# An attention whose TensorE order is written out in steps: score bank, third transposes, weighted sum, projections, second score bank, first two transposes

## The chip, the cores and the metric

The kernel runs on one NeuronCore of a Trainium2 chip. The metric is the device time of one execution in microseconds (us). Three executions of the kernel before took 912.99, 913.64 and 913.80 us; the median is 913.64 us. The profile is of one more execution.

## The reference, cut to what matters

Two layers over 1040 tokens (16 meta tokens and 1024 real ones) with 1024 features: a multi-head latent attention, then a recurrent mixer. Only the attention is touched by the change. For each of 8 heads it computes

```
s = (einsum('bqhd,bkhd->bhqk', qn, k_nope) + einsum('bqhr,bkr->bhqk', qr, k_rope)) * scale
s = where(mask, s, MASK_VALUE)          # causal
p = softmax(s, axis=-1)
out = einsum('bhqk,bkhd->bqhd', p, v)
y = out.reshape(B, T, MLA_WIDTH) * silu(gate)
return y @ w_out
```

where q, k and v are projections of normalised latents (384 features for q, 256 for k and v).

## The kernel before

**Precision.** Nearly every product is made of three matmuls in the type fp32r on a high and a low part of each operand (`mm3`: high*high, high*low, low*high). So each result that feeds another product is copied out of PSUM by ScalarE (`hi_of`, the high part), and VectorE then writes the difference (`lo_of`, the low part). A PSUM bank is free for the next product when that difference is done.

**Stages.** Input projection and gate come first (to about 206 us in the trace), then the attention (206 to 513 us), then the output projection and the second layer.

**The attention.** A head is cut into 9 blocks of 116 queries (`QBLK`, the last has 112); a unit is (head h, block t), 72 units in all. Names in the trace:

- `pk`, `pqn`, `pv`: the projections `k_unit`, `q_unit`, `v_unit`. Keys and queries come in chunks of 348 tokens, three to a head, values in 9 blocks for a pair of heads. They share two PSUM banks (tag "g") with the weighted sum `o`, and become `kh`/`kl`, `qh`/`ql`, `v`.
- `s`: `scores(h, t)`, five matmuls for each segment of keys, up to two segments in a tile of two banks; there are two such tiles (tag "s2"). Only t = 8 needs a second tile (1040 keys in three segments), so `s..8_0` and `s..8_1` take both. VectorE adds the causal mask and takes the row minimum `m`; ScalarE writes the exponential `p` out of the tile (L523), which frees it. For t = 8 the minimum spans both tiles, so neither exponential starts before `s..8_1` is done. There are three buffers of `p`, so the exponential of unit u+3 also waits for the transposes of unit u.
- `pt`: `transposes(h, t)` turns `p` over in groups of up to three 116x116 transposes, a group to each chunk of keys (one group for t = 0 to 2, two for 3 to 5, three for 6 to 8). There are two banks for groups (tag "t"). ScalarE and VectorE copy a group to `pth` and `ptl`; a bank is free after `ptl`.
- `o`: `weighted(h, g)`, once after every third unit, 9, 18 or 27 matmuls over a chunk of 348 queries.

**Order.** The loop runs over the units: scores of the unit three ahead (`LEAD`), a pending weighted sum, the projections that a table assigns to this unit (`fill`), the transposes of this unit. It only states dependencies and priority: a scheduler that knows the program places the instructions of every engine, and TensorE executes them in that order. It pulls pieces apart: between the matmuls of one weighted sum stand scores, transposes and projections. At odd heads `load_pair` also brings the projection weights of the next two heads, which ScalarE and VectorE split (`h_wkv`, `h_wq`, `l_wq`); `h_wq` goes into the buffer of the old weights, so it can only start when the last `pqn` of the pair has read them. In head 7 there is no next head; instead the output weights `wa` are split and three tiles of the output projection (`ao`) are placed there.

**At the start**, `k_unit(0,0)`, `k_unit(0,1)`, `q_unit(0,0)` follow each other, and ScalarE loads its table for exponentials behind the last gate.

Of the kernel before, what the change touches and what calls it, by code (L numbers as in the profile page):

```python
# [62 lines left out]
def trunk(ctx, tc, x, meta, a_norm_g, a_w_in, a_q_g, a_kv_g, a_w_uq, a_w_ukv, a_w_out,  # L63
# [18 lines left out]
    def lo_of(dst, src, hi):  # L82
        return nc.vector.tensor_tensor(dst, src, bc(hi), ALU.subtract)  # L83

    def mm3(ps, lh, ll, rh, rl, start, stop, **kw):
        nc.tensor.matmul(ps, lh, rh, start=start, stop=False, **kw)  # L86
        nc.tensor.matmul(ps, lh, rl, start=False, stop=False, **kw)  # L87
        return nc.tensor.matmul(ps, ll, rh, start=False, stop=stop, **kw)  # L88

    def mm_stack(ps, xp, k, n, wh, wl):  # L90
        if k:
            nc.tensor.matmul(ps[:n], xp[:, k, :n], wl, start=False, stop=False)
        nc.tensor.matmul(ps[:STK + n], xp[:, k], wh, start=k == 0, stop=k == KT - 1)
        if not k:
            nc.tensor.matmul(ps[:n], xp[:, k, :n], wl, start=False, stop=False)

# [70 lines left out]
    def transpose_in(xn, n, t0, xth, xtl, name):  # L167
        for j in range(2):
            pt = ps_t(f"xt_{name}_{j}")
            pv = pt.rearrange("p (a b) -> p a b", b=P)[:, :, :n]  # L170
            for a in range(4):
                k = 4 * j + a
                nc.tensor.transpose(pv[:, a], xn[:n, k * P:(k + 1) * P], ident[:n, :n])
# [120 lines left out]
    def lat_post(i, lt, krf):  # L294
        t0, n = TOK[i]
        pt = ps_t(f"qt{i}")
        pv = pt.rearrange("p (a b) -> p a b", b=P)[:, :, :n]
        for a in range(QKT):
            nc.tensor.transpose(pv[:, a], lt[:, a * P:(a + 1) * P], ident[:n, :n])
        nc.tensor.transpose(pv[:, 3], krf[:, 0:P], ident[:n, :n])  # L300
        hi_of(qlh[:, :, t0:t0 + n], pv[:, :3])
        lo_of(qll[:, :, t0:t0 + n], pv[:, :3], qlh[:, :, t0:t0 + n])
        nc.scalar.activation(ks1[:, t0:t0 + n], pv[:, 3], AF.Copy)
        pt = ps_t(f"kt{i}")
        pv = pt.rearrange("p (a b) -> p a b", b=P)[:, :, :n]
        for a in range(VKT):
            nc.tensor.transpose(pv[:, a], lt[:, QL + a * P:QL + (a + 1) * P], ident[:n, :n])
        nc.tensor.transpose(pv[:, 2], krf[:, DR:DR + P], ident[:n, :n])
# [19 lines left out]
    for c in range(0, D, 512):  # L328
        ps = ps_m(f"rb_ga{c}")
        nc.tensor.matmul(ps, ones, g_a[0:1, c:c + 512], start=True, stop=True)  # L330
        rbs.append(ps)
# [109 lines left out]
    def k_unit(h, c):  # L441
        if c == 0:
            KK[h] = (pat.tile([P, T], F32R, name=f"kh{h}", tag="kh", bufs=2),
                     pat.tile([P, T], F32R, name=f"kl{h}", tag="kl", bufs=2))
        kvw, hh = KV[h // 2], h % 2
        c0, cw = CH[c]
        ps = ps_g(f"pk{h}_{c}")[:, :cw]
        for k in range(VKT):
            last = mm3(ps, kvw[0][:, k, hh * 256:hh * 256 + DN], kvw[1][:, k, hh * 256:hh * 256 + DN],
                       klh[:, k, c0:c0 + cw], kll[:, k, c0:c0 + cw], k == 0, k == VKT - 1)  # L450
        kh, kl = KK[h]
        hi_of(kh[:, c0:c0 + cw], ps)
        lo_of(kl[:, c0:c0 + cw], ps, kh[:, c0:c0 + cw])
        return last

# [29 lines left out]
    def scores(h, t):  # L485
# [13 lines left out]
        for s, sg in enumerate(tiles):  # L499
            ps2 = ps_2(f"s{h}_{t}_{s}")  # L500
            w = sg[0][1]
            for j, (k0, w_) in enumerate(sg):
                assert w_ == w
                ps = ps2[:n, j, :w]
                nc.tensor.matmul(ps, a, kth[:, k0:k0 + w], start=True, stop=False)  # L505
                nc.tensor.matmul(ps, a, ktl[:, k0:k0 + w], start=False, stop=False)
                nc.tensor.matmul(ps, b_, kth[:, k0:k0 + w], start=False, stop=False)
                nc.tensor.matmul(ps, r_, ks1[:, k0:k0 + w], start=False, stop=False)
                nc.tensor.matmul(ps, r_, ks2[:, k0:k0 + w], start=False, stop=True)  # L509
# [23 lines left out]

    def transposes(h, t):
        g = t // 3
        b0, n = QBLK[t]
        off = b0 - CH[g][0]
        p = PP.pop((h, t))
        if t % 3 == 0:
            PT[h, g] = [(pat.tile([QB, GRP, CHW], F32R, name=f"pth{h}_{g}_{tr}", tag="pth", bufs=3),  # L540
                         pat.tile([QB, GRP, CHW], F32R, name=f"ptl{h}_{g}_{tr}", tag="ptl", bufs=3))
                        for tr in range(g + 1)]
        for tr in range(g + 1):
            pth, ptl = PT[h, g][tr]
# [3 lines left out]
            for j, kb in enumerate(kbs):  # L548
                k0, nk = QBLK[kb]
                nc.tensor.transpose(pv[:nk, j], p[:, k0:k0 + nk], ident[:n, :n])  # L550
            nfull = sum(1 for kb in kbs if QBLK[kb][1] == QB)
# [97 lines left out]
    for h in range(H):  # L649
        for c in range(len(CH)):  # L650
# [33 lines left out]
    for u in range(LEAD):  # L684
        scores(*units[u])
# [12 lines left out]
    st_at.close()  # L698
# [445 lines left out]
```

## Time and profile before

| what | us |
|---|---|
| median of three executions | 913.64 |
| profiled execution, whole time | 913.04 |
| its span on the core | 911.3 |
| TensorE (PE) matmuls busy in the span | 887.8 |
| VectorE (DVE) busy | 582.9 |
| ScalarE (ACT) busy | 467.7 |

The span is the time between the first and the last instruction; 1.7 us lie around it. PE is TensorE's matmul side, PEld its weight loads, POOL GpSimd and SP the queue that issues DMAs. A matmul's duration in the trace runs until its last result has left the array, so matmuls that follow each other overlap; the distance of their starts tells how long each holds the engine. The granted TensorE clock is a share of 2.4 GHz.

### The profile page before, as it was taken

The page shows a single profiled execution, that of the slowest core. Times are in us where ns is not written, and L with a number is a line of the kernel's source. Part 1 is how long each engine was busy: PE and PEld are TensorE (multiplying, and loading weights), DVE is VectorE, ACT ScalarE, POOL GpSimd, SP SyncE. Part 2 cuts the span into 40 slices and gives each one's busy share as a digit, 9 for nine tenths or more (in the row PEclk, how much of TensorE's full clock was granted, in tenths as well). Part 3 has the DMA queues.
Part 4 walks back from the last instruction along what each step waited for, and adds up shares of the span by engine and source line. Part 5 has one row for each costly group of instructions (what it writes and reads, how often), then busy time and mean ns, then how long its engine had stood idle before and what let it go on. Part 6 is the DMA issues. An engine that isn't in the chain of part 4 may idle for free.

```text
span 911.3 us, 13708 instructions
## 1 busy us (share of the span) xinstructions
PE 887.8 (97%) x5291; PEld 817.2 (90%) x5291; DVE 582.9 (64%) x1211; ACT 467.7 (51%) x942; POOL 43.6 (5%) x46
## 2 busy tenths in 40 slices
PE   7999999999999999999999999999999999999996
PEld 5999999999999999999988778799989989897885
DVE  6675423416677676676777357757393764868997
ACT  6543422224665655656656235634835457365455
POOL 3000000000000000000000000000020110312200
PEclk9999999999999999999999999999999999999998
DMA  7132345221010010010012424241111121237624
GB/s 275 48 87 64 85 110 158 73 72 40 16 57 16 17 55 16 17 63 16 17 37 103 163 92 159 101 75 48 46 47 51 43 58 36 95 90 231 141 68 184
DMA packets 71169, 72.25 MB, mean 79 GB/s; under 512 B 15056, under 2 KB 52688, under 8 KB 71104
## 3 DMA queue, kind: packets, MB, share of 16 engines
q1 hardware_dynamic: 68928, 67.19, 23.8%
q0 software_dynamic: 2176, 4.19, 2.6%
q8 instruction: 41, 0.67, 0.3%
q14 instruction: 24, 0.20, 0.1%
HBM read 58.65 MB, written 12.71 MB: 78 GB/s over the span
## 4 chain that ended last, share of the span: by engine, by line
PE 92%; ACT 3%; DVE 2%; issue 1%; DMA 0%; ACTq 0%; DVEq 0%
PE pt L550 4%; PE pu L88 3%; PE pu L86 3%; PE pu L87 3%; PE ga L86 3%; PE ao L86 3%; PE ga L87 3%; PE ga L88 3%; PE ao L88 3%; PE ao L87 3%; PE pg L87 3%; PE pg L88 3%; PE pg L86 3%; PE s L505 2%; PE b L86 2%; PE b L88 2%
## 5 line engine op out<-in xcount | busy, mean ns | idle before, releaser
L523 ACT ACTIVATE p<-s,m 116x116 f32<-116x116 f32 (+4 forms) x80 | 55.4, 694 | 45.1 <-DVE m L515 16.5
L80 ACT ACTIVATE pth<-pt 116x348 fp32r<-116x348 f32 (+5 forms) x152 | 57.1, 397 | 29.7 <-PE pt L550 26.2
L83 DVE TENSOR_TENSOR ptl<-pt,pth 116x348 fp32r<-116x348 f32 (+5 forms) x152 | 63.7, 437 | 9.7 <-ACT pth L80 9.2
L88 PE MATMUL pu<-x2h,l_wu 128*128 128x348 f32 (+1 forms) x192 | 61.5, 321 | 0.4 <-DVE l_wu L83 0.4
L86 PE MATMUL ga<-xth,h_wg 128*128 128x348 f32 (+1 forms) x192 | 61.9, 322 | 0.0
L86 PE MATMUL pu<-x2h,h_wu 128*128 128x348 f32 (+1 forms) x192 | 61.7, 322 | 0.0
L87 PE MATMUL pu<-x2l,h_wu 128*128 128x348 f32 (+1 forms) x192 | 61.7, 321 | 0.0
L87 PE MATMUL ga<-xtl,h_wg 128*128 128x348 f32 (+1 forms) x192 | 61.6, 321 | 0.0
L88 PE MATMUL ga<-xth,l_wg 128*128 128x348 f32 (+1 forms) x192 | 61.6, 321 | 0.0
L515 DVE CUSTOM_DVE_ANT_0 s<-s,maskt 116x116 f32<-116x116 f32 (+8 forms) x72 | 49.4, 686 | 16.9 <-PE s L509 16.6
L550 PE MATMUL pt<-ident,p 116*116 116x116 f32 (+1 forms) x360 | 54.0, 262 | 1.0 <-DVE ptl L83 0.6
L86 PE MATMUL ao<-wah,yh_a 128*128 128x512 f32 x128 | 50.5, 396 | 0.6 <-DVE Y L574 0.6
L87 PE MATMUL pg<-x2l,h_wbg 128*128 128x512 f32 x128 | 50.6, 395 | 0.0
L88 PE MATMUL pg<-x2h,l_wbg 128*128 128x512 f32 x128 | 50.3, 393 | 0.0
L86 PE MATMUL pg<-x2h,h_wbg 128*128 128x512 f32 x128 | 50.2, 392 | 0.0
L88 PE MATMUL ao<-wah,yl_a 128*128 128x512 f32 x128 | 50.2, 393 | 0.0
L87 PE MATMUL ao<-wal,yh_a 128*128 128x512 f32 x128 | 49.8, 390 | 0.0
L505 PE MATMUL s<-kh,qh 128*116 128x348 f32 (+7 forms) x120 | 42.0, 350 | 6.5 <-ACT p L523 6.5
L550 PEld LDWEIGHTS pt<-ident,p 116*116 116x116 f32 (+1 forms) x360 | 41.5, 135 | 4.0 <-PE pt L550 1.5
L87 PE MATMUL o<-ptl,v 116*128 116x348 f32 (+1 forms) x144 | 45.1, 313 | 0.0
L86 PE MATMUL o<-pth,v 116*128 116x348 f32 (+1 forms) x144 | 43.2, 300 | 0.8 <-ACT pth L80 0.8
L88 PE MATMUL o<-pth,v 116*128 116x348 f32 (+1 forms) x144 | 44.0, 305 | 0.0
(328 smaller groups left out, 2652.7 us busy)
## 6 DMA issues: line engine op xcount, KB each, us to landing
wg<-in_a_w_in SPq DMA_DIRECT2D x8, 512.0 KB, 3.9
wa<-in_a_w_out SPq DMA_DIRECT2D x8, 512.0 KB, 3.5
wu<-in_b_w_in SPq DMA_DIRECT2D x8, 512.0 KB, 4.0
wbg<-in_b_w_in SPq DMA_DIRECT2D x8, 512.0 KB, 4.0
hr<-hscr SPq DMA_DIRECT2D x8, 512.0 KB, 8.2
out_h<-hr SPq DMA_DIRECT2D x16, 256.0 KB, 2.1
x<-in_x SPq DMA_DIRECT2D x7, 512.0 KB, 3.5
wq<-in_b_w_out SPq DMA_DIRECT2D x6, 512.0 KB, 3.5
```

The source lines that it names most:

```text
L80: return nc.scalar.activation(dst, src, AF.Copy)
L83: return nc.vector.tensor_tensor(dst, src, bc(hi), ALU.subtract)
L86: nc.tensor.matmul(ps, lh, rh, start=start, stop=False, **kw)
L87: nc.tensor.matmul(ps, lh, rl, start=False, stop=False, **kw)
L88: return nc.tensor.matmul(ps, ll, rh, start=False, stop=stop, **kw)
L505: nc.tensor.matmul(ps, a, kth[:, k0:k0 + w], start=True, stop=False)
L515: MKD[h, t] = nc.vector.tensor_tensor_reduce(pv, pv, mk, 1.0, -NEG, ALU.add, ALU.min, m[:, s:s + 1])
L523: MK[h, t] = nc.scalar.activation(dst, pv, AF.Exp, bias=mx, scale=-1.0, accum_out=l[:, s:s + 1])
L550: nc.tensor.transpose(pv[:nk, j], p[:, k0:k0 + nk], ident[:n, :n])
```

## The change

Every TensorE instruction is now issued through `pe_mm` or `pe_tr`, which remember the last one. In the loop each step is issued behind that last instruction (`next_pe`), so that the scheduler can no longer pull steps apart. `scores` becomes a generator that stops after the first tile when there is a second. `transposes` takes the list of its groups.

A unit's steps are then: first score tile of the unit three ahead; third transposes of the unit before; pending weighted sum; projections; second score tile, if there is one; first two groups of transposes of this unit. In the last unit the transposes come ahead of the projections. The query projection moves to the front of its unit's list. At the start, the query projection comes between the two key projections, and the load of ScalarE's table comes behind the copy of the first key projection.

```diff
+    def pe_mm(*a, **kw):
+        PE_LAST[0] = nc.tensor.matmul(*a, **kw)
+        return PE_LAST[0]
...
             pss.append((pv, p[:, k0:k0 + ns * w].rearrange("p (a b) -> p a b", a=ns)))
+            if s + 1 < len(tiles):
+                yield
...
-    def transposes(h, t):
+    def transposes(h, t, trs):
...
-        for tr in range(g + 1):
+        for tr in trs:
...
-                fill[units[u + 1]].append(lambda h=h, c=c: q_unit(h, c))
+                fill[units[u + 1]].insert(0, lambda h=h, c=c: q_unit(h, c))
...
-    behind([silu], nc.scalar.activation, warm, ones[:, 0:1], AF.Exp)
-    k_unit(0, 0)
-    ku = k_unit(0, 1)
-    behind([ku], q_unit, 0, 0)
+    first_k = behind([silu], k_unit, 0, 0)
+    behind([first_k], nc.scalar.activation, warm, ones[:, 0:1], AF.Exp)
+    q_unit(0, 0)
     for u in range(-LEAD - 2, 0):
         for c in (1, 2):
-            if 3 * c - LEAD - 2 == u and c > 1:
+            if 3 * c - LEAD - 2 == u:
                 k_unit(0, c)
...
+    def next_pe(f, *a):
+        behind([PE_LAST[0]], f, *a)
+
+    back = None
     for u, (h, t) in enumerate(units):
-        if u + LEAD < len(units):
-            scores(*units[u + LEAD])
+        sc = scores(*units[u + LEAD]) if u + LEAD < len(units) else iter(())
+        next_pe(next, sc, None)
+        if back:
+            next_pe(transposes, *back)
+            back = None
         if pending:
-            weighted(*pending)
+            next_pe(weighted, *pending)
             pending = None
+        end = u + 1 == len(units)
+        if end:
+            next_pe(transposes, h, t, range(2))
         for f in fill[h, t]:
-            f()
-        transposes(h, t)
+            next_pe(f)
+        next_pe(next, sc, None)
+        if not end:
+            next_pe(transposes, h, t, range(min(t // 3 + 1, 2)))
+        if t // 3 == 2:
+            back = (h, t, (2,))
         if t % 3 == 2:
             pending = (h, t // 3)
+    transposes(*back)
     weighted(*pending)
```

What that does to the order is seen at three places. In the names, the first number is the head, the second the unit's block or the chunk, the third the score tile or the group of transposes.

**Place 1, TensorE, the end of head 1's scores.** Before, the last matmul of `s1_8_1` is followed by a weighted sum and a value projection, of which the first rows are:

```order
L509 MATMUL s1_8_1_2978<-ks2_87,qr1_2_2858 112x344
L86 MATMUL o1_1_3032<-pth1_1_0_2895,v0_0_2251 128x348
L86 MATMUL pv1_0_3087<-h_wkv2_2929,klh_93 116x256
L87 MATMUL pv1_0_3087<-l_wkv2_2930,klh_93 116x256
L88 MATMUL pv1_0_3087<-h_wkv2_2929,kll_94 116x256
```

In all, nine matmuls of `o1_1`, two value projections and two groups of transposes stand there ahead of head 2's first scores, `s2_0_0`. Now `s2_0_0` follows `s1_8_1` after six transposes:

```order
L88 MATMUL s1_8_1_2994<-ks1_86,qr1_2_2858 112x344
L88 MATMUL s1_8_1_2994<-ks2_87,qr1_2_2858 112x344
L92 MATMUL pt1_5_0_3007<-ident_78,p1_5_2828 116x116 x3
L92 MATMUL pt1_5_1_3013<-ident_78,p1_5_2828 116x116 x3
L88 MATMUL s2_0_0_3022<-kh2_2941,qh2_0_2988 116x116
```

On ScalarE the same place reads, after the change:

```order
L475 ACTIVATE qh2_0_2988<-pqn2_0_2978 128x348
L80 ACTIVATE pth1_1_0_2895<-pt1_5_0_3007 116x3x116
L80 ACTIVATE pth1_1_1_2897<-pt1_5_1_3013 116x3x116
L535 ACTIVATE p1_8_2965,l1_8_2964<-s1_8_0_2966,m1_8_2963 112x696
L535 ACTIVATE p1_8_2965,l1_8_2964<-s1_8_1_2994,m1_8_2963 112x344
L541 ACTIVATE p1_8_2965<-p1_8_2965,l1_8_2964 112x1040
```

`s2_0_0` takes the tile of `s1_8_0`; the work that stood ahead of it on TensorE has moved behind it, and both copies of `pt1_5` stand ahead of the exponential that frees the tile.

**Place 2, TensorE, the last query projection of head 1.** Before, its last matmul is followed by a weighted sum and by the scores of block 5:

```order
L88 MATMUL pqn1_2_2844<-qlh_91,l_wq0_2188 128x344
L87 MATMUL o0_2_2759<-ptl0_2_2_2621,v0_6_2502 128x344
L88 MATMUL o0_2_2759<-pth0_2_2_2620,v0_6_2502 128x344
L86 MATMUL o0_2_2759<-pth0_2_2_2620,v0_7_2658 128x228
L87 MATMUL o0_2_2759<-ptl0_2_2_2621,v0_7_2658 128x228
L88 MATMUL o0_2_2759<-pth0_2_2_2620,v0_7_2658 128x228
L505 MATMUL s1_5_0_2829<-kh1_2505,qh1_1_2720 116x348
```

Now three transposes stand between it and the scores that use it:

```order
L88 MATMUL pqn1_2_2844<-qlh_91,l_wq0_2188 128x344
L92 MATMUL pt1_2_0_2860<-ident_78,p1_2_2684 116x116 x3
L88 MATMUL s1_6_0_2869<-kh1_2505,qh1_2_2854 116x406
L88 MATMUL s1_6_0_2869<-kl1_2506,qh1_2_2854 116x406
L88 MATMUL s1_6_0_2869<-kh1_2505,ql1_2_2855 116x406
```

The scores of block 5 and the weighted sum have moved ahead of the projection.

**Place 3, TensorE, the three groups of transposes of unit (1, 7).** Before, the nine matmuls of a query projection stand between the second and the third group, the last three of them here:

```order
L86 MATMUL pqn2_1_3156<-qlh_91,h_wq2_2937 128x348
L87 MATMUL pqn2_1_3156<-qll_92,h_wq2_2937 128x348
L88 MATMUL pqn2_1_3156<-qlh_91,l_wq2_2938 128x348
L550 MATMUL pt1_7_2_3128<-ident_78,p1_7_2911 116x116 x2
L550 MATMUL pt1_8_0_3172<-ident_78,p1_8_2965 116x112 x3
```

Now five score matmuls do:

```order
L92 MATMUL pt1_7_0_3116<-ident_78,p1_7_2911 116x116 x3
L92 MATMUL pt1_7_1_3122<-ident_78,p1_7_2911 116x116 x3
L88 MATMUL s2_2_0_3131<-kh2_2941,qh2_0_2988 116x348
L88 MATMUL s2_2_0_3131<-kl2_2942,qh2_0_2988 116x348
L88 MATMUL s2_2_0_3131<-kh2_2941,ql2_0_2989 116x348
L88 MATMUL s2_2_0_3131<-ks1_86,qr2_0_2992 116x348
L88 MATMUL s2_2_0_3131<-ks2_87,qr2_0_2992 116x348
L92 MATMUL pt1_7_2_3141<-ident_78,p1_7_2911 116x116 x2
```

The third group uses the bank of the first; the nine matmuls between them have moved behind it, and the five of a score tile have come in.

## Rows read from the trace of the kernel before

**Rows 1.** The page's first part: busy us, share of the span, instructions.

```profile
PE 887.8 (97%) x5291; PEld 817.2 (90%) x5291; DVE 582.9 (64%) x1211; ACT 467.7 (51%) x942; POOL 43.6 (5%) x46
```

**Rows 2.** Windows: length, busy PE, PEld, DVE, ACT, POOL; PEclk, DMA share, GB/s.

```profile
206.00:513.00 307.00, 297.93 (x2028) 283.57 (x2028) 212.12 (x569) 177.34 (x437) 0.20 (x1) 1.00 0.12 39
...
900.00:911.00 11.00, 3.87 (x29) 3.50 (x27) 5.88 (x20) 4.98 (x15) 0.00 (x0) 0.79 0.53 196
```

**Rows 3.** Waits of TensorE, 205 to 513 us: total us, times, longest.

```profile
PE s L505 <- ACT p L523: 6.5, 9, 1.0
PE pqn L86 <- DVE kl L83: 1.7, 1, 1.7
PE o L86 <- ACT pth L80: 0.8, 2, 0.6
PE pt L550 <- DVE ptl L83: 0.6, 2, 0.5
...
PEld s L505 <- ACT p L523: 8.6, 9, 1.3
...
PEld pt L550 <- PE pt L550: 1.5, 4, 0.7
```

**Rows 4.** Timeline, end of a head's scores: start, us, engine, line, operation.

```profile
340.23 1.03 ACT L523 ACTIVATE p<-s,m 116x928 f32<-116x928 f32 x1 [0.56 <-PE pt L550]
...
341.40 0.41 PE L505 MATMUL s<-kh,qh 128*112 128x344 f32 x1 [0.92 <-ACT p L523]
...
342.13 0.32 PE L509 MATMUL s<-ks,qr 128*112 128x344 f32 x1
...
343.11 0.16 DVE L521 TENSOR_TENSOR m<-m 112x1 f32<-112x1 f32 x1
...
343.67 0.84 ACT L523 ACTIVATE p<-s,m 112x696 f32<-112x696 f32 x1
```

**Rows 5.** Timeline of a group of transposes and the bank that it waits for.

```profile
317.75 0.46 ACT L465 ACTIVATE qh<-pqn 128x348 fp32r<-128x348 f32 x1 [0.48 <-PE pqn L88]
317.93 0.39 DVE L83 TENSOR_TENSOR ptl<-pt,pth 116x232 fp32r<-116x232 f32 x1
318.11 0.45 ACT L80 ACTIVATE pth<-pt 116x336 fp32r<-116x336 f32 x1
...
318.47 0.48 PE L550 MATMUL pt<-ident,p 112*116 112x112 f32 x3 [0.47 <-DVE ptl L83]
...
318.98 0.45 ACT L80 ACTIVATE pth<-pt 116x336 fp32r<-116x336 f32 x1 [0.43 <-PE pt L550]
...
319.47 0.51 DVE L83 TENSOR_TENSOR ptl<-pt,pth 116x336 fp32r<-116x336 f32 x1 [0.29 <-ACT pth L80]
```

**Rows 6.** Timeline of the last query projection of an odd head.

```profile
254.34 0.32 PE L87 MATMUL pqn<-qll,h_wq 128*128 128x344 f32 x1
...
254.49 0.32 PE L88 MATMUL pqn<-qlh,l_wq 128*128 128x344 f32 x1
...
255.44 0.44 ACT L465 ACTIVATE qh<-pqn 128x344 fp32r<-128x344 f32 x1
...
256.44 0.51 DVE L466 SCALAR_TENSOR_TENSOR ql<-pqn,qh 128x344 fp32r<-128x344 f32 x1
```

**Rows 7.** Timeline of a value projection: its last matmul and its split.

```profile
314.72 0.28 PE L88 MATMUL pv<-h_wkv,kll 128*112 128x256 f32 x1
...
315.45 0.42 DVE L83 TENSOR_TENSOR v<-pv,v 112x256 fp32r<-112x256 f32 x1
```

**Rows 8.** Timeline of ScalarE and of VectorE in head 7.

```profile
473.64 0.46 ACT L465 ACTIVATE qh<-pqn 128x344 fp32r<-128x344 f32 x1 [1.61 <-PE pqn L88]
...
478.95 0.50 DVE L83 TENSOR_TENSOR ptl<-pt,pth 116x348 fp32r<-116x348 f32 x1
```

**Rows 9.** Timeline of the attention's start.

```profile
203.33 0.32 PE L86 MATMUL pk<-klh,h_wkv 128*128 128x348 f32 x1
203.35 0.96 DVE L83 TENSOR_TENSOR l_wq<-wq,h_wq 128x768 fp32r<-128x768 f32 x1 [9.99 <-ACT h_wq L80]
```

More of the change, by code (lines that the diff above doesn't have):

```diff
@@ L83, in lo_of, with pe_tr @@
         return nc.vector.tensor_tensor(dst, src, bc(hi), ALU.subtract)
+    PE_LAST = [None]
+    def pe_mm(*a, **kw):
+        PE_LAST[0] = nc.tensor.matmul(*a, **kw)
+        return PE_LAST[0]
+    def pe_tr(*a):
+        PE_LAST[0] = nc.tensor.transpose(*a)
+        return PE_LAST[0]
     def mm3(ps, lh, ll, rh, rl, start, stop, **kw):
-        nc.tensor.matmul(ps, lh, rh, start=start, stop=False, **kw)
-        nc.tensor.matmul(ps, lh, rl, start=False, stop=False, **kw)
-        return nc.tensor.matmul(ps, ll, rh, start=False, stop=stop, **kw)
+        pe_mm(ps, lh, rh, start=start, stop=False, **kw)
+        pe_mm(ps, lh, rl, start=False, stop=False, **kw)
+        return pe_mm(ps, ll, rh, start=False, stop=stop, **kw)
     def mm_stack(ps, xp, k, n, wh, wl):
         if k:
-            nc.tensor.matmul(ps[:n], xp[:, k, :n], wl, start=False, stop=False)
-        nc.tensor.matmul(ps[:STK + n], xp[:, k], wh, start=k == 0, stop=k == KT - 1)
+            pe_mm(ps[:n], xp[:, k, :n], wl, start=False, stop=False)
+        pe_mm(ps[:STK + n], xp[:, k], wh, start=k == 0, stop=k == KT - 1)
         if not k:
-            nc.tensor.matmul(ps[:n], xp[:, k, :n], wl, start=False, stop=False)
+            pe_mm(ps[:n], xp[:, k, :n], wl, start=False, stop=False)
     cst = ctx.enter_context(tc.tile_pool(name="cst", bufs=1))
@@ L172, in transpose_in @@
                 k = 4 * j + a
-                nc.tensor.transpose(pv[:, a], xn[:n, k * P:(k + 1) * P], ident[:n, :n])
+                pe_tr(pv[:, a], xn[:n, k * P:(k + 1) * P], ident[:n, :n])
             hs = xth[:, 4 * j:4 * j + 4, t0:t0 + n]
@@ L298, in lat_post @@
         for a in range(QKT):
-            nc.tensor.transpose(pv[:, a], lt[:, a * P:(a + 1) * P], ident[:n, :n])
-        nc.tensor.transpose(pv[:, 3], krf[:, 0:P], ident[:n, :n])
+            pe_tr(pv[:, a], lt[:, a * P:(a + 1) * P], ident[:n, :n])
+        pe_tr(pv[:, 3], krf[:, 0:P], ident[:n, :n])
         hi_of(qlh[:, :, t0:t0 + n], pv[:, :3])
@@ L306, in lat_post @@
         for a in range(VKT):
-            nc.tensor.transpose(pv[:, a], lt[:, QL + a * P:QL + (a + 1) * P], ident[:n, :n])
-        nc.tensor.transpose(pv[:, 2], krf[:, DR:DR + P], ident[:n, :n])
+            pe_tr(pv[:, a], lt[:, QL + a * P:QL + (a + 1) * P], ident[:n, :n])
+        pe_tr(pv[:, 2], krf[:, DR:DR + P], ident[:n, :n])
         hi_of(klh[:, :, t0:t0 + n], pv[:, :2])
@@ L329, in trunk @@
         ps = ps_m(f"rb_ga{c}")
-        nc.tensor.matmul(ps, ones, g_a[0:1, c:c + 512], start=True, stop=True)
+        pe_mm(ps, ones, g_a[0:1, c:c + 512], start=True, stop=True)
         rbs.append(ps)
@@ L448, in k_unit @@
         for k in range(VKT):
-            last = mm3(ps, kvw[0][:, k, hh * 256:hh * 256 + DN], kvw[1][:, k, hh * 256:hh * 256 + DN],
+            mm3(ps, kvw[0][:, k, hh * 256:hh * 256 + DN], kvw[1][:, k, hh * 256:hh * 256 + DN],
                        klh[:, k, c0:c0 + cw], kll[:, k, c0:c0 + cw], k == 0, k == VKT - 1)
         kh, kl = KK[h]
-        hi_of(kh[:, c0:c0 + cw], ps)
+        mark = hi_of(kh[:, c0:c0 + cw], ps)
         lo_of(kl[:, c0:c0 + cw], ps, kh[:, c0:c0 + cw])
-        return last
+        return mark
     def q_unit(h, c):
@@ L504, in scores @@
                 ps = ps2[:n, j, :w]
[L505 to L509, printed above, removed]
+                pe_mm(ps, a, kth[:, k0:k0 + w], start=True, stop=False)
+                pe_mm(ps, a, ktl[:, k0:k0 + w], start=False, stop=False)
+                pe_mm(ps, b_, kth[:, k0:k0 + w], start=False, stop=False)
+                pe_mm(ps, r_, ks1[:, k0:k0 + w], start=False, stop=False)
+                pe_mm(ps, r_, ks2[:, k0:k0 + w], start=False, stop=True)
             ns, k0 = len(sg), sg[0][0]
@@ L537, in transposes @@
         off = b0 - CH[g][0]
-        p = PP.pop((h, t))
-        if t % 3 == 0:
+        p = PP[h, t]
+        if t % 3 == 0 and 0 in trs:
             PT[h, g] = [(pat.tile([QB, GRP, CHW], F32R, name=f"pth{h}_{g}_{tr}", tag="pth", bufs=3),
@@ L549, in transposes @@
                 k0, nk = QBLK[kb]
-                nc.tensor.transpose(pv[:nk, j], p[:, k0:k0 + nk], ident[:n, :n])
+                pe_tr(pv[:nk, j], p[:, k0:k0 + nk], ident[:n, :n])
             nfull = sum(1 for kb in kbs if QBLK[kb][1] == QB)
```

2 lines of the change are left out of this document (1 added, 1 removed).

## The prediction

> **What bounds the kernel now.** I read the page first: TensorE is busy 97% of the span, and no other engine is above 64% [rows 1]. Then the table of stages: the change lies in the attention, 206 to 513 us, where TensorE shows 297.9 busy of 307 us, while VectorE and ScalarE have 95 and 130 us to spare [rows 2]. So TensorE sets the end: any time in which it stands is paid in full, and any time in which it stood and no longer stands is gained. The question is therefore only which waits go and which come. Then the waits of TensorE in that stretch: fourteen, nine of them scores waiting for the exponential that frees their tile [rows 3]. Last the timelines around each kind of place that the new order makes.
>
> The idle times there understate what a wait costs. A matmul of 344 columns has a row of 0.32 us but the next starts 0.15 us later [rows 6]; a wait is counted from the row's end, some 0.16 us after the engine could have gone on. I use that pitch, scaled by columns, and 0.1 us for one transpose.
>
> **What goes.** The nine waits of scores, the one at the start, two of a weighted sum and two of transposes make 6.5 + 1.7 + 0.8 + 0.6 = 9.6 us [rows 3]. With 14 times 0.16 that is 11.8 us, and the four short waits that only the weight loads show add 1.5 us [rows 3]: 13.3 us. Most of their places don't exist in the new order, and I let all of them go. That is the most that the change can gain, since the instructions of TensorE stay the same in number and kind. The Trainium skill holds matmul busy time for a bad measure of headroom and takes the time of the weight loads instead (Perfetto Trace Analysis, Identifying the Most-Contended Engine). By that, 307 - 283.6 = 23.4 us would be open here [rows 2], and the sum below would end 10 us lower.
>
> **What comes.** I time each new wait from the order of the change and rows of this trace.
>
> *Scores of the next head (heads 0 to 6).* Let t be the start of the last matmul of s..8_1. Six transposes follow, and TensorE comes to the next head's scores at t + 0.76. Their tile is that of s..8_0. The row minimum is ready at t + 1.14 (from 342.13 to the end of the row at 343.11, [rows 4]). But ScalarE does the two copies of the transposes first. A copy starts 0.51 after the first transpose of its group, and one copy follows another after 0.36 [rows 5], so they start at t + 0.67 and t + 1.03, and the exponential at t + 1.39. It takes 0.84, and the scores start 0.14 after an exponential's end [rows 4]: t + 2.37. That is a wait of 1.6 us, seven times: 11.2 us. Bounds: the nearest wait of the trace, at 341.40, has 0.92 idle and so 1.1 us, with no copy ahead of the exponential [rows 4]; a query split that holds VectorE first gives 1.9.
>
> *Third transposes (t = 6 and 7, heads 0 to 6).* There are two banks, and the third group takes the first group's. From the first group's start f, the copy begins at f + 0.51, the difference 0.49 later, takes 0.51, and the next group starts some 0.15 after it [rows 5]: f + 1.66. On TensorE lie six transposes and five score matmuls. At t = 6 (232 columns) it is there at f + 1.15, a wait of 0.5. At t = 7 (348 columns) it is there at f + 1.4, but a key projection just ahead takes ScalarE and VectorE first, which puts the bank's end to f + 1.8: 0.4. At t = 8 (464 columns) f + 1.65 hides it. Together 7 x 0.9 = 6.3 us. Bounds: 0.25 each if the copies are met by idle engines at their best, 0.63 as at 318.47 (0.47 idle [rows 5]).
>
> *Scores behind the query projection (odd heads).* Let k be the start of its last matmul; TensorE comes to the scores at k + 0.46, after three transposes. In heads 1, 3 and 5 ScalarE splits the next weights first and qh ends at k + 1.39, ql at k + 2.46 [rows 6]. Before, a weighted sum and the scores of block 5 covered that. Now the first matmul waits until k + 1.54, which is 1.1 us; the third needs ql, and a scaling of about 0.45 that now stands ahead of it on VectorE puts it to k + 3.05 against k + 1.92: another 1.1. Head 7 has no weights to split: 0.7. Together 3 x 2.2 + 0.7 = 7.3 us. Bounds: 4 (only qh waits) to 8.5. At even heads a value projection lies between; there it costs nothing at the scores, and about 0.15 us at the weighted sum behind them, whose copy now follows an exponential: 0.6 us.
>
> *Key projection behind two value projections (heads 1, 3, 5).* It takes the bank of the first, free 1.15 us after that one's last matmul [rows 7], 1.3 with the release; the second covers 0.83. 3 x 0.47 = 1.4 us.
>
> *Head 7.* ScalarE and VectorE split the output weights behind qh, in the same order as before, and the difference of the transposes of block 2 ends 5.8 us after qh's start [rows 8]. Before, scores and output matmuls stood there. Now the first weighted sum follows one score tile and needs it 2.8 us after that start: 3.1 us. The second weighted sum follows its transposes directly, 0.9 us; two third groups follow theirs directly, 1.06 each. Together 6.1 us.
>
> *Start.* The query projection comes first and meets its split weights: l_wq ends at 204.31, the third matmul could start at 203.65 [rows 9], so 0.8 us with the release; 0.2 at the third scores. 1.0 us.
>
> Sum: 11.2 + 6.3 + 7.3 + 0.6 + 1.4 + 6.1 + 1.0 = 33.9 us. DMA, POOL and the stages outside stay as they are; the query scratch loads are issued as early as before and cost nothing.
>
> The Trainium skill says that TensorE's queue pulls weight loads ahead of matmuls in flight (TensorE: Matmul & The Clock Gate, the table at its top). A wait would then end without a load. The trace doesn't show it at these waits: at the same nine the loads stood 8.6 us and the matmuls 6.5 [rows 3], so the loads waited too. By the rule each of some 35 new waits is 0.1 shorter, and the time 3.5 us lower.
>
> **The sum.** 913.04 (profiled execution) - 13.3 + 33.9 = 933.6; the median of the runs stands 0.6 above the profiled one, so 934.
>
> **Rivals.**
>
> *The banks come free in time (faster).* The old score waits go, and the new waits stay at their cheapest: 1.1 us at the next head's scores, none at the transposes, 0.5 at the queries and 1.5 elsewhere: 7.7 + 2 + 1.5 = 11.2, so about 911; if the exponential also ran ahead of both copies, some 908. It decides where the new waits sum to less than 13.3 us. For it: ScalarE has 130 us to spare, and spread score tiles are what the old waits ask for. Against it: the order of ScalarE is fixed, and both copies, and the weights, stand ahead.
>
> *The waits only change places (no change).* New waits of 12 to 15 us, for instance 1.1 at the scores, 0.25 at each third group and half of what I have in head 7: 913. Against it: every one of these bounds would have to hold at once.
>
> *The clock falls too (slower still).* In the last stretch, where TensorE is busy 3.87 of 11 us, the granted clock is 0.79, between the levels of 2.4 and 1.2 GHz [rows 2]; in the attention it is 1.00 though single waits reach 1.7 us [rows 2, 3]. If the longer waits (3.1 in head 7, two of 1.1 close together at the odd heads, seven of 1.6) lower it, a microsecond of matmuls at the lower level costs one more; two of them behind each of eight waits give 16 us, and 950.
>
> That the order isn't what the change says is no rival: the built order has the steps as written, with the one limit that only t = 8 has a second score bank.
>
> **How the numbers follow.** Forecast 934, with a chance of 0.80; its own range from the bounds: low, 7 x 1.1 + 14 x 0.25 + 4 + 1.4 + 3.5 + 0.5 = 20.6, less 13.3, gives 921; high, 7 x 1.9 + 14 x 0.63 + 8.5 + 2 + 7 + 2 = 41.6, less 13.3, gives 942. Faster 0.07; no change 0.06; clock 0.04; 0.03 for waits that I don't see. The range for 8 in 10 reaches from 918 to 942. A measurement tells about 0.2%, 1.8 us, from no change. Slower by over that: 0.87; within: 0.06; faster: 0.07.
>
> **What would show it.** In the waits of TensorE after: scores waiting for the exponential seven times with some 1.4 us idle, in the rows right behind the transposes of t = 5; pt waiting for ptl some 14 times and more; scores waiting for qh and ql in heads 1, 3, 5; one wait of 3 us of a weighted sum for ptl in head 7; TensorE's idle time in the attention at some 25 us instead of 9. The old waits, at 341.40 and its like [rows 4], should be gone. The prediction is wrong where the scores of a next head start within 0.3 us of the transposes, or where third groups follow without idle time. A granted clock below 1.00 in the attention would speak for the last rival.

## The result, and the profile after

The changed kernel takes **941.35 us** (median of four runs, 938.99 to 943.9) against 913.37 for the kernel before in the same comparison: a ratio of 1.0306, 95% interval 1.0281 to 1.033. It is 28 us slower. The forecast was 934, with a range of 918 to 942. The direction and most of the amount came as forecast; some 7 us came on top.

First the page's first part for the changed kernel, the profiled run of 938.99 us (span 937.2):

```profile
PE 897.1 (96%) x5291; PEld 820.5 (88%) x5291; DVE 583.8 (62%) x1211; ACT 470.3 (50%) x942; POOL 43.8 (5%) x46
```

The number of instructions is that of [rows 1] on every engine, so nothing was added; TensorE shows 9.3 us more busy time with the same matmuls. That is the first hint at something that isn't a wait. Next the windows (length, busy time of PE, PEld, DVE, ACT and POOL, granted clock, DMA share, GB/s): the attention as a whole, and then cut around three short places:

```profile
206.00:541.00 335.00, 308.45 (x2034) 287.89 (x2033) 213.50 (x569) 180.40 (x438) 0.21 (x1) 0.98 0.12 37
206.00:236.00 30.00, 28.19 (x194) 26.78 (x192) 20.88 (x58) 17.41 (x44) 0.00 (x0) 1.00 0.11 30
236.00:241.00 5.00, 5.00 (x28) 5.00 (x28) 0.92 (x5) 1.45 (x3) 0.00 (x0) 0.66 0.00 0
241.00:393.50 152.50, 140.50 (x966) 132.60 (x964) 101.49 (x276) 85.43 (x213) 0.00 (x0) 1.00 0.09 28
393.50:398.00 4.50, 4.50 (x25) 4.50 (x24) 0.71 (x4) 1.41 (x2) 0.00 (x0) 0.62 0.00 0
...
499.50:504.50 5.00, 4.60 (x20) 4.27 (x21) 4.44 (x8) 2.48 (x7) 0.00 (x0) 0.66 0.71 229
```

The last matmul of the last weighted sum starts at 538.04 us here and at 512.13 in the trace of before: the attention takes 25.9 us more, which is the whole loss of the profiled run (938.99 against 913.04). What lies ahead of it and behind it kept its length; this window reaches 2 us further beyond the attention than that of [rows 2]. Its idle TensorE time went from 9 to 27 us, and in three places the granted clock fell to the lower of its two levels. In [rows 2] it was 1.00 throughout. Now the waits of TensorE in the attention (total us, times, longest), to be read against [rows 3]:

```profile
PE s L88 <- ACT p L535: 10.0, 7, 1.4
PE pt L92 <- DVE ptl L83: 4.6, 12, 1.2
PE o L88 <- DVE ptl L83: 3.1, 6, 1.3
PE s L88 <- ACT qh L475: 2.7, 4, 0.8
PE s L88 <- DVE ql L476: 2.6, 3, 0.9
PE o L88 <- ACT pth L80: 1.6, 2, 1.3
PE pk L88 <- DVE v L83: 0.7, 3, 0.2
...
```

The old waits for the exponential are gone, the place at 341.40 of [rows 4] among them, and every row here is one that the prediction named. The largest, seven scores waiting for the exponential, stands at one place, the end of each head's scores (timeline: start, duration, engine, operation, idle time ahead in brackets):

```profile
234.12 0.81 ACT L80 ACTIVATE pth<-pt 116x348 fp32r<-116x348 f32 x2 [0.62 <-PE pt L92]
...
234.82 0.84 ACT L535 ACTIVATE p<-s,m 112x696 f32<-112x696 f32 x1
...
235.81 0.31 PE L88 MATMUL s<-kh,qh 128*116 128x116 f32 x1 [1.43 <-ACT p L535]
```

Both copies of the transposes run first on ScalarE, then the exponential, and TensorE stands for 1.43 us. Compare 343.67 in [rows 4]: the same exponential, with work under it on TensorE.

### The profile page after: what moved, and what is told of

The parts are those of the page before. It is cut to its first block, busy times and chain, and to the rows that moved or that the text cites. A ratio compares the mean times of both kernels' runs of the same rounds, so it can differ in the third digit from the quotient of the medians.

```text
span 937.2 us, 13713 instructions
## 1 busy us (share of the span) xinstructions
PE 897.1 (96%) x5291; PEld 820.5 (88%) x5291; DVE 583.8 (62%) x1211; ACT 470.3 (50%) x942; POOL 43.8 (5%) x46
## 4 chain that ended last, share of the span: by engine, by line
PE 88%; DVE 5%; ACT 4%; DMA 1%; issue 1%; DVEq 0%; ACTq 0%; SPq 0%
PE ao L88 10%; PE pu L88 10%; PE pg L88 9%; PE ga L88 9%; PE s L88 9%; PE b L88 7%; PE o L88 7%; PE pk L88 6%; PE pz L88 5%; PE pq L88 4%; PE pqn L88 4%; PE pt L92 3%; PE pv L88 2%; PE qr L88 2%; ACT p L535 1%; DVE ptl L83 1%
## 5 line engine op out<-in xcount | busy, mean ns | idle before, releaser
L88 PE MATMUL o<-pth,v 116*128 116x344 f32 (+5 forms) x288 | 68.5, 315 | 1.6 <-ACT pth L80 1.6
L535 ACT ACTIVATE p<-s,m 116x116 f32<-116x116 f32 (+4 forms) x80 | 55.6, 698 | 26.2 <-PE pt L92 18.2
L88 PE MATMUL s<-ks,qr 128*116 128x348 f32 (+7 forms) x240 | 58.3, 324 | 0.0
L88 PE MATMUL s<-kh,qh 128*116 128x348 f32 (+7 forms) x120 | 44.1, 368 | 12.7 <-ACT p L535 10.0
L88 PEld LDWEIGHTS o<-pth,v 116*128 116x128 f32 (+1 forms) x288 | 52.2, 198 | 2.2 <-ACT pth L80 2.1
```

Of the source, the lines that this page charges most:

```text
L88: PE_LAST[0] = nc.tensor.matmul(*a, **kw)
L535: MK[h, t] = nc.scalar.activation(dst, pv, AF.Exp, bias=mx, scale=-1.0, accum_out=l[:, s:s + 1])
```

## The experiments

One measure serves all of them. For each TensorE instruction of the attention I take the distance to the next one's start and subtract the median distance for the same output tile and shape; what is left, if over 0.2 us, counts as a wait. The count runs from the first key projection to the first matmul behind the last weighted sum. So counted, the kernel before has 13.7 us of waits and the changed one 34.5. Theory A says that the time is a fixed base, plus these waits, plus a price for each stretch at half rate. Theory B says that the clock has nothing to do with the waits; theory C that the waits are a symptom and the fixed order costs by itself, on the other engines.

**The second weighted sum ahead of the scores.**

```diff
+        if t == 6 and pending:
+            next_pe(weighted, *pending)
+            pending = None
         next_pe(next, sc, None)
```

> The changed kernel with one step put back: at t = 6 of heads 0 to 6 the second weighted sum (o_1) goes ahead of the next head's first score tile. Theory A (each new wait costs its own stand, and TensorE's clock falls behind the longer ones): the seven waits of scores for the exponential, 1.59 us each, go (11.1 us); the sum now directly follows its transposes and waits for their copies as it does in head 7 of the changed kernel, 0.88 us each (6.2 us). Two of the three stretches at the lower clock stood behind the waits that go, 1.7 us each. Net 5 us from the waits and 0 to 6 us from the clock: 930 to 936, with a granted clock of 1.00 around these places. Theory B (the waits explain the sum, the clock is a thing of its own): 936, with stretches at half rate as before. Theory C (it is the fixed order on the other engines that costs, not this wait): within 1 us of the changed kernel, 941.

It took 933.89 us (932.55 to 935.29; ratio 1.0229, 1.0212 to 1.0246), 7.5 less than the changed kernel. The seven waits of 1.59 us for the exponential went, and the weighted sum waited for its copies instead, twice some 0.42 us in each head. The waits fell by 5.2 us in all. In the profiled run two stretches at half rate were left, and one of them at a new place. This is the wait of the scores for the query's second half in head 3, which ends at 336.44, and the window behind it, where the granted clock is 0.53:

```profile
330.00:336.90 6.90, 5.20 (x33) 4.58 (x33) 5.98 (x14) 4.74 (x10) 0.00 (x0) 1.00 0.34 108
336.90:340.30 3.40, 3.40 (x14) 3.27 (x13) 1.65 (x3) 0.00 (x0) 0.00 (x0) 0.53 0.40 148
```

The same wait in the changed kernel's profiled run had no such stretch behind it. So the waits' part of theory A holds, and the clock isn't tied to one place. Theory B had 936 here; 2 us are too little to settle it.

**The third groups of transposes spread.**

```diff
+        if h + 1 < H and t >= 7:
+            if t == 8:
+                next_pe(transposes, h, 7, (1,))
+            next_pe(fill[h, t][0])
+            next_pe(transposes, h, t - 1, (2,))
+            for f in fill[h, t][1:]:
+                next_pe(f)
+            next_pe(transposes, h, t, (0,))
+            back, pending = ((h, 8, (1, 2)), (h, 2)) if t == 8 else (None, None)
+            continue
```

> The changed kernel with the transposes of t = 6, 7 and 8 of heads 0 to 6 set apart, so that between any two groups that use the same bank some 1.7 us of TensorE work lie: the third group of t = 6 behind the first projection of t = 7, the second group of t = 7 behind the next score tile, and so on. Theory A: the waits of third groups, 0.42 and 0.30 us by start against start, go: 5 us less, and less again by what the clock gave up behind them; no large change of the stretches at half rate, since those stood behind other waits: 934 to 937. The risk is that the exponentials, which need the buffer that the transposes read last, come later: then scores wait for them in heads 1 to 7, and nothing is won, 941. Theory C (the order on the other engines): 941, with the waits of transposes gone and others in their place.

933.83 us (933.28 to 937.13; 1.0232, 1.0214 to 1.025). The fourteen waits of 0.42 and 0.30 us went, one of 0.26 us came in the even heads, 4.6 us less in all; the median lies just under the 934 to 937 expected. In the profiled run (933.28) two stretches at half rate stood where the waits for the exponential had been left as they were, in heads 0 and 4. The exponentials did not come late.

**The last query projection of a head one step earlier.**

```diff
-                fill[units[u + 1]].insert(0, lambda h=h, c=c: q_unit(h, c))
+                if c < 2:
+                    fill[units[u + 1]].insert(0, lambda h=h, c=c: q_unit(h, c))
+                else:
+                    fill[units[u]].append(lambda h=h, c=c: q_unit(h, c))
```

> The changed kernel with one projection moved: the query projection of the third chunk of each head goes one step earlier, behind the key projection of that chunk (t = 1 and not t = 2). Theory A: the waits of the scores of block 6 for qh and ql, 2.03 us in heads 1, 3 and 5 and 0.41 in head 7, go: 6.5 us; a weighted sum behind those scores may then wait 0.5 us in the odd heads as it does in the even ones, which gives back 2: 4.5 to 6.5 us less, 935 to 937. Theory C: 941.

928.99 us (1.0172, 1.0134 to 1.0211): more than expected, and with a gap between its runs. Two took 925.7 and 925.86 us at a mean granted clock of 0.998, which is where the runs of the kernel before lie (0.997 to 0.999); the other two took 932.12 and 932.65 at 0.991. The profile is of the 932.12 run, and it shows four stretches at half rate. Two of them, and the stretch ahead of the first:

```profile
230.00:236.80 6.80, 5.38 (x38) 5.13 (x38) 4.54 (x15) 5.04 (x13) 0.00 (x0) 1.00 0.11 26
236.80:240.30 3.50, 3.50 (x17) 3.50 (x16) 0.13 (x1) 1.08 (x1) 0.00 (x0) 0.54 0.00 0
274.40:277.80 3.40, 3.40 (x18) 3.40 (x17) 0.52 (x1) 0.76 (x2) 0.00 (x0) 0.53 0.00 0
```

The same kernel, and 6.6 us between the means of its two pairs of runs: with four stretches in the traced run of the slower pair, and none in the faster one as its granted clock suggests, that is 1.65 us for each. The first expectation had put that price at 1.7. The waits fell by 8.3 us: of the 6.5 expected 5.8 went (0.24 us stayed in heads 1, 3 and 5), and the 0.54 us of the weighted sum in the even heads went too.

**The wait for the exponential filled, nothing moved.**

```diff
+        if t == 6 and h + 1 < H:
+            next_pe(idle_mm, *pending)
         next_pe(next, sc, None)
```

Here `idle_mm` issues ten matmuls into the bank of the weighted sum that comes next; that sum overwrites their result.

> The changed kernel with extra work and nothing moved: at t = 6 of heads 0 to 6, ahead of the next head's first score tile, ten matmuls of 348 columns whose result is overwritten by the weighted sum that comes next in the same bank (they are work that the kernel doesn't need). Ten times 0.15 us fill the wait of 1.6 us, so the scores start when they did. Theory A (the clock falls because TensorE stood): the stretches at half rate behind these places go, two of the three of the profiled run; 3.4 us less than the changed kernel in its fastest run and up to 6 less in its slower ones, 935 to 938, with less spread between runs. Theory B (the falls have nothing to do with these waits): the same 939 to 944 with the same spread. If the ten matmuls aren't hidden, 941 plus up to 11.

938.8 us (935.96 to 939.27; 1.0272, 1.0256 to 1.0288), 0.8 above what theory A allowed and 2.5 below the changed kernel. In the profiled run (935.96) the two stretches in heads 0 and 4 were gone and the one in head 7 was still there, behind waits that this kernel left. The other three runs are 2 to 3 us slower at a lower mean granted clock (0.993 and 0.994 against 0.996); they were not traced, and that other waits lowered the clock in them is likely but not shown. So this run alone decides little.

**All long waits filled, nothing moved.** The same with 13 matmuls ahead of the scores of block 6 in heads 1, 3 and 5, 3 in head 7, and 20, 6, 7 and 9 at head 7's long waits.

```diff
+        if t == 6:
+            next_pe(idle_mm, 10 if h + 1 < H else 6, (h, 1))
+        if t == 3 and h % 2:
+            next_pe(idle_mm, 13 if h + 1 < H else 3, (h, 0))
         next_pe(next, sc, None)
+        if t == 3 and h + 1 == H:
+            next_pe(idle_mm, 20, (h, 0))
+        if t == 7 and h + 1 == H:
+            next_pe(idle_mm, 7)
+        if t == 8 and h + 1 == H:
+            next_pe(idle_mm, 9)
```

> The changed kernel with nothing moved and extra matmuls that the kernel doesn't need in every wait of 0.8 us or more: 10 of 348 columns ahead of each next head's first scores, 13 ahead of block 6's scores in heads 1, 3 and 5 (3 in head 7), and in head 7 20 ahead of the first weighted sum, 6 ahead of the second, 7 and 9 ahead of the third groups of t = 6 and 7. At 0.15 us each they take as long as the waits did, so the sum of waits is the same and TensorE hardly stands. Theory A: no stretch at half rate is left, each run at 934 plus or minus 1, with runs within 1 us of each other: 7 us below the changed kernel, which is then the price of the clock alone. Theory B (the clock falls for another reason): 939 to 944 with the old spread. If the matmuls take longer than the waits they add up to some 3 us.

935.66 us (934.88 to 936.39; 1.0238, 1.0223 to 1.0254). A kernel with 154 matmuls more is 5.7 us faster, and its runs lie within 1.5 us of each other, where those of the changed kernel lie within 4.9. First a filled wait in its timeline, then the attention in its windows:

```profile
234.42 1.84 PE L88 MATMUL o<-ks,ks 128*128 128x348 f32 x10
...
235.09 0.85 ACT L535 ACTIVATE p<-s,m 112x696 f32<-112x696 f32 x1
...
236.10 0.29 PE L88 MATMUL s<-kh,qh 128*116 128x116 f32 x1
```

```profile
206.00:537.00 331.00, 324.90 (x2191) 307.57 (x2190) 213.27 (x569) 180.30 (x438) 0.21 (x1) 1.00 0.12 38
```

The scores still start right behind the exponential; TensorE does useless work ahead of them, and the granted clock is 1.00 from end to end of the attention. The mean granted clocks of the four runs, 0.997 to 0.999, are those of the kernel before, so the three that were not traced give no sign of a stretch either. That is against theory B: take away TensorE's standing, leave the order, and the lower level goes. The median is 0.7 us above what theory A allowed, since the extra matmuls may themselves add a little. What the clock cost the changed kernel is then 941.35 - 935.66 = 5.7 us or somewhat more; by the ratios to the kernel before, each taken beside its own runs, it is 1.0306 - 1.0238, or 6.2 us.

**Every new wait given cover, first try.** Second weighted sum, key projection, query projection and transposes moved together; in head 7 the splits of the output weights come later, and two of the output tiles are cut in halves. Pieces of the edit:

```diff
+        if t == 7 and not last:
+            next_pe(fs.pop())
+        if t == 6:
+            next_pe(weighted, h, 1)
         next_pe(next, sc, None)
...
+        if t in (1, 2):
+            tr(h, t, 0)
+        if t == 5:
+            tr(h, t, 0, 1)
...
-        fill[H - 1, t].append(lambda kk=kk: behind([MK[H - 1, (4, 4, 5, 5)[kk]]], part_out, kk))
+        fill[H - 1, t].append(lambda kk=kk: behind([MK[H - 1, (5, 5, 6, 6)[kk]]], part_out, kk))
```

> The changed kernel with its steps set in another order, so that each of the new waits gets work ahead of it: the second weighted sum ahead of the next head's first score tile, and the transposes of t = 5 ahead of the query projection and of the second score tile; the third groups spread as in the run with spread transposes; the third chunk's query projection one step earlier; the key projection of t = 7 ahead of the value projections; in head 7 the output weights' splits behind the exponentials of blocks 5 and 6, and the two last output tiles of the attention cut in halves between the groups of transposes. Theory A (waits plus the clock behind them, nothing else): without any stretch at half rate the changed kernel would be 934.0 (938.99 less three times 1.65); the waits that go are 11.2 (scores for the exponential), about 7.5 of 8.1 (third groups), 6.1 (weighted sums), 6.5 (scores for the query halves) and 1.2 (key projections), 32.5 us in all; 901 to 905, runs close together and the granted clock at 1.00 in the attention, 8 to 12 us faster than the kernel before. Theory C (an order fixed by hand costs TensorE by itself): 913 or above.

927.21 us (1.0142, 1.0125 to 1.0159), far above the 901 to 905 that theory A expected. Its waits:

```profile
PE pt L92 <- DVE ptl L83: 12.6, 13, 3.1
PE s L88 <- DVE ql L476: 5.1, 3, 1.7
PE pv L88 <- DVE kl L83: 1.7, 3, 0.6
...
```

Other waits of the same kind have come up. Seven of 1.24 us by starts stand at t = 5, where I had moved the transposes ahead:

```profile
230.67 1.04 ACT L535 ACTIVATE p<-s,m 116x928 f32<-116x928 f32 x1
...
231.68 0.37 ACT L80 ACTIVATE pth<-pt 116x232 fp32r<-116x232 f32 x1
...
232.07 0.88 DVE L527 TENSOR_REDUCE m<-s 112x1 f32<-112x696 f32 x1
232.87 0.39 DVE L83 TENSOR_TENSOR ptl<-pt,pth 116x232 fp32r<-116x232 f32 x1
...
233.41 0.49 PE L92 MATMUL pt<-ident,p 116*116 116x116 f32 x3 [1.07 <-DVE ptl L83]
```

The second group of t = 5 takes the bank of the second group of t = 4. That one's copy stands behind block 7's exponential on ScalarE, its difference behind a row minimum of 0.88 us on VectorE, and the bank comes free only with the difference. In head 7 a single wait of 3.3 us stood behind the splits of the output weights. The time alone is what theory C expected, 913 or above. But the waits are there to be counted, 25.0 us, with two stretches at half rate, so it takes an order without them to tell the two theories apart.

**Second try, with those places mended.** At t = 5 both score tiles come first, then the transposes, the query projection and the weighted sum; in head 7 one output weight is split behind each of four exponentials, with its difference on GpSimd (the `True` below). The run beside it keeps the changed kernel's splits, on VectorE. Pieces of the edit, against the first try:

```diff
-        for a, b in zip(A0["w"], load_wo(A0["pwo"], a_w_out, 0, "wa", 4, (kk,), kk in ())):
+        for a, b in zip(A0["w"], load_wo(A0["pwo"], a_w_out, 0, "wa", 4, (kk,), True)):
...
+    for kk, t in enumerate((3, 3, 3, 4)):
+        fill[H - 1, t].append(lambda kk=kk: behind([MK[H - 1, 4 + kk]], part_out, kk))
...
-        if t in (1, 2):
-            tr(h, t, 0)
         if t == 5:
-            tr(h, t, 0, 1)
...
+            next_pe(next, sc, None)
+            tr(h, 5, 0, 1)
...
-        if t == 0 or t >= 7 and not last:
+        if t < 3 or t >= 7 and not last:
             tr(h, t, 0)
```

> A second reordering after the run with all waits covered, which got 927 because new waits came up: 15.7 us of transposes behind their banks (1.24 in each head at t = 5, where a scaling and an exponential on ScalarE stood ahead of the copy; 4.6 in head 7 behind the splits of the output weights), 5.5 of scores for the query's second half in the odd heads (the weight split stood ahead on VectorE), 2.1 of a value projection. Here t = 5 goes both score tiles, six transposes, query projection, weighted sum, next head's scores; t = 1 has the projections ahead of the transposes as in the run with the early query; in head 7 one output weight is split behind each of four exponentials, its difference on GpSimd. Theory A (waits plus clock): of the 24.7 us of waits in that run some 20 go, so 903 to 908, and no stretch at half rate where no wait of 1 us is left. Theory D (ScalarE and VectorE have no room: whatever order TensorE gets, some copy stands behind an exponential and the waits only move): 913 to 925, with new waits of the same kind in other places.

> The same reordering, but the output weights are split as in the changed kernel (two behind the exponential of block 4, two behind that of block 5 of head 7, differences on VectorE). Theory A: the heads 0 to 6 as in the other run of this pair, and head 7 again with some 3 us of a weighted sum's wait behind the splits and the clock's share behind it: 3 to 6 us above the other run, 907 to 913. If GpSimd's subtractions cost more than they save, it is the other way round.

The first took **908.42 us** (907.85 to 909.17), a ratio of 0.9945 to the kernel before, interval 0.9929 to 0.9962: it beats both kernels, by 5.3 and by 33 us, and lies 0.4 above what theory A expected. The second took 910.92 (0.9973, 0.9961 to 0.9985), 2.5 more where 3 to 6 were expected; a wait of 2.7 us of head 7's first weighted sum is there, with a stretch at half rate behind it. Waits and attention of the first:

```profile
PE pt L92 <- DVE ptl L83: 3.6, 9, 1.2
PE ao L88 <- DVE Y L586: 0.6, 1, 0.6
PE pqn L88 <- DVE l_wq L83: 0.4, 1, 0.4
```

```profile
206.00:508.00 302.00, 296.99 (x2027) 282.45 (x2025) 207.87 (x564) 180.43 (x437) 9.95 (x5) 1.00 0.13 39
```

Every step of these two is issued behind TensorE's last instruction, as in the changed kernel. So theory C falls: the fixed order costs nothing by itself, and this one is faster than the scheduler's. The rival that ScalarE and VectorE have no room falls for heads 0 to 6, whose waits are down to pieces of under 0.4 us; in head 7 two of 1.4 and 1.0 us remain.

**The balance.** With the 1.65 us for a stretch at half rate from the run with the early query, the profiled runs give:

| kernel | time, us | waits | stretches | time less both |
|---|---|---|---|---|
| before | 913.04 | 13.7 | 0 | 899.4 |
| changed | 938.99 | 34.5 | 3 | 899.5 |
| sum ahead of scores | 932.73 | 29.3 | 2 | 900.1 |
| third groups spread | 933.28 | 29.9 | 2 | 900.1 |
| query early | 932.12 | 26.2 | 4 | 899.3 |
| first reordering | 927.59 | 25.0 | 2 | 899.3 |
| second reordering | 908.19 | 9.0 | 0 | 899.2 |
| the same, splits on VectorE | 911.14 | 10.3 | 1 | 899.2 |

The two kernels with extra matmuls join them if each of these is counted at its pitch of 0.16 us: 935.96 - 23.4 - 1.65 - 70 x 0.16 = 899.7, and 934.88 - 10.4 - 154 x 0.16 = 899.8. Ten kernels, one base, to within 0.9 us. In part that is bookkeeping: inside the attention the distances between starts add up to its length by themselves. What the balance adds is that the pitch of the instructions, losses under 0.2 us each and the stages outside the attention account for no difference over 0.9 us between the kernels. That the waits come from the order, and the lower clock from waits, rests on the experiments above, the filled waits and the second reordering first of all.

## Why the prediction was right, and where it was short

**What bounds the kernel.** Right. TensorE sets the end, and each wait of it was paid in full; behind some of them the lower clock was paid on top.

**What goes, 13.3 us.** Right: 12.9 us by starts without the wait of the output tile (`ao`), which both kernels have, 0.77 us in each.

**Scores of the next head, 1.6 us seven times.** Right to the hundredth: 1.59 in all seven. The order of ScalarE decided it, as worked out.

**Third transposes, 0.5 and 0.4.** 0.42 and 0.30, so 5.0 us and not 6.3; t = 8 was hidden as said.

**Scores behind the query projection, 1.1 and 1.1 in odd heads, 0.7 in head 7.** 0.99, 1.04 and 0.41: 6.5 us and not 7.3. The rows of head 1, to be laid beside [rows 6]: the split of the next weights ahead of qh on ScalarE, and ahead of ql on VectorE.

```profile
259.56 0.84 ACT L80 ACTIVATE h_wq<-wq 128x768 fp32r<-128x768 f32 x1 [0.83 <-PE pqn L88]
...
260.30 0.44 ACT L475 ACTIVATE qh<-pqn 128x344 fp32r<-128x344 f32 x1
260.43 0.96 DVE L83 TENSOR_TENSOR l_wq<-wq,h_wq 128x768 fp32r<-128x768 f32 x1 [0.17 <-ACT h_wq L80]
...
260.80 0.44 PE L88 MATMUL s<-kh,qh 128*116 128x406 f32 x1 [0.82 <-ACT qh L475]
...
261.74 0.51 DVE L476 SCALAR_TENSOR_TENSOR ql<-pqn,qh 128x344 fp32r<-128x344 f32 x1
...
262.30 0.44 PE L88 MATMUL s<-kh,ql 128*116 128x406 f32 x1 [0.88 <-DVE ql L476]
```

**The weighted sum at even heads, 0.15 us four times.** Mis-sized: 0.54, so 2.2 us and not 0.6. I had looked at the copy on ScalarE; the late one was the difference, behind a scaling on VectorE:

```profile
223.03 0.58 DVE L543 TENSOR_SCALAR p<-p,l 116x696 f32<-116x696 f32 x1
...
223.52 0.51 DVE L83 TENSOR_TENSOR ptl<-pt,pth 116x348 fp32r<-116x348 f32 x1
...
224.09 0.42 PE L88 MATMUL o<-ptl,v 116*128 116x348 f32 x1 [0.39 <-DVE ptl L83]
```

**Key projection, 0.47 three times.** 0.38. **Head 7, 6.1 us.** 6.9: the first weighted sum as said, 1.46 + 1.61 us, the second 0.88, the two third groups 1.01 and 1.38, and 0.54 us behind the last that I hadn't seen. The first weighted sum's rows, whose splits are those of [rows 8] in a new place:

```profile
497.97 2.00 ACT L80 ACTIVATE wah<-wa 128x1024 fp32r<-128x1024 f32 x2
498.13 0.43 PE L88 MATMUL o<-pth,v 116*128 116x348 f32 x1 [1.30 <-ACT pth L80]
...
499.35 0.50 DVE L83 TENSOR_TENSOR ptl<-pt,pth 116x348 fp32r<-116x348 f32 x1
...
499.90 0.49 PE L88 MATMUL o<-ptl,v 116*128 116x348 f32 x1 [1.34 <-DVE ptl L83]
```

**Start, 1.0 us.** 0.57.

**The sum.** 33.4 us of new waits measured in these terms, 33.9 forecast: the misses cancel, and that is luck. The profiled run less its three stretches is 938.99 - 3 x 1.65 = 934.0, against 933.6 in the sum for a profiled execution. The changed kernel never ran that fast, and the term that the sum lacked is the clock: three stretches in the profiled run make 5 us, and the other runs, with mean granted clocks of 0.991, 0.989 and 0.987 against its 0.993, are slower in that order (940.51, 942.18, 943.9).

The step that failed is the last rival, *The clock falls too*. It had the mechanism, and the number was wrong in two ways. I set it as a case apart, at 950 with a chance of 0.04, where it should have been a term of the likeliest case. Its evidence against was that the clock stood at 1.00 in the attention of before *though single waits reach 1.7 us*; but that wait is a single one at the attention's start [rows 3], and the other old waits are at most 1.13 us by starts. The new order has fourteen of a microsecond or more. And I priced it at eight places with 2 us each. The profiled run shows three places, at some 1.65 us each; in the other three runs, where each 0.002 less of the mean granted clock goes with 1.5 to 1.7 us, I estimate four to six. Taken as a term of 5 to 10 us it would have put the forecast at 939 to 944. As it was, the range held the median by 0.65 us only, and for another reason than those that set its upper end: that it held is luck.

**The rivals of the other sign.** That banks come free in time, or that waits only change places, was refuted by the waits themselves: of the large terms none stood at its lower bound, and the sum, 33.4 us, lies far above the 11 to 15 us that these rivals needed. Only the key projections' 1.2 us came in under their 1.4.

**The two rules that I weighed.** The Trainium skill (Perfetto Trace Analysis, Identifying the Most-Contended Engine) would have had 23.4 us open in the attention of before. The runs show what is open there: 13.7 us of waits. The best order here got 5 us of them, with weight loads of 282.45 us in a window of 302, and the base of the balance leaves the attention some 293 us, not 284. The Trainium skill's other rule, that weight loads are pulled ahead (TensorE: Matmul & The Clock Gate, the table at its top), again doesn't show at these waits. In the row of the weight loads that answers to the seven waits for the exponential (it counts eight loads), the loads stood longer than the matmuls' 10.0 us:

```profile
PEld s L88 <- ACT p L535: 11.7, 8, 1.6
```

## What to carry to other kernels

An order written out by hand is as good as the cover that it gives each wait: for every step that reads a bank or a copy, list what runs on TensorE between the step that starts the chain (transposes, projection, scores) and the one that needs its end, and hold it against the other engines' time in their own order, splits and scalings included. Sum these waits from starts of instructions, not from idle time. Where a reordering brings many waits like those here (fourteen of 1.0 to 1.6 us, where there had been five) into a stretch that had few, add a term for the clock, and widen the range for its scatter; where runs of one kernel differ by 0.2% and more, look at the mean granted clock of each run before anything else.

## What the runs showed of the hardware

I had not expected the clock's choice of places. Each of the fifteen stretches at half rate in the attentions of the profiled runs began within 2.1 us of the end of a wait of 1.0 to 3.3 us by starts, but most such waits had none behind them: the seven of 1.59 us are alike to 0.01 us in every head, and in the changed kernel's profiled run the clock fell behind those of heads 0 and 4 only, in the run with the early query behind those of heads 0 and 1. The kernel before has five waits of 1.1 to 1.8 us, the second reordering two of 1.0 and 1.4 us, and neither has a stretch. Inside a stretch the same matmul row is half as long again, `o` with 348 columns 0.49 us instead of 0.32, and the starts lie 0.29 us apart instead of 0.16. What picks the wait isn't settled by these runs. That useless matmuls in the waits make a kernel faster by 5.7 us was new to me too, though the better use of the knowledge is to put useful ones there.
